# Gates and results of a dense FFN loaded in a step of their own, three chunks ahead, with four places each

## The chip, the cores and the metric

The kernel runs on one core of one Trainium2 chip. The metric is the device time of one execution in microseconds (us), lower is better. Engines are named as in the profile: PE (TensorE matmuls), PEld (TensorE weight loads), DVE (VectorE), ACT (ScalarE), POOL (GpSimd) and SP (SyncE, which issues nearly all loads and stores of this kernel; its rows read SPq). L714 is line 714 of the kernel.

## The reference

A two-layer diffusion transformer for 256 latent and 256 context tokens of width 1024. Each layer has an attention mixer and then a PEER feed-forward part: a product-key router picks 16 of 16,384 experts for each of 8 heads, each expert being one row of `u` and one row of `v`.

```python
idx = jnp.take_along_axis(cand_i.reshape(PEER_CHUNK, PEER_HEADS, PEER_TOPK * PEER_TOPK), best_j, axis=-1)
g = jax.nn.softmax(best_s, axis=-1)
a = jnp.einsum('td,thkd->thk', t, u[idx])
w = (jax.nn.gelu(a.astype(jnp.float32)) * g).astype(t.dtype)
return jnp.einsum('thk,thkd->td', w, v[idx])
```

In layer 0 this is done for latent and context tokens, in layer 1 (the last) for latent tokens alone.

## The kernel before

**Dense experts.** The kernel does not gather experts for the latent tokens. It writes a table of gates (tokens by 16,384 experts, mostly zeros) to DRAM, multiplies the tokens with all of `u` (the U stage), multiplies the results elementwise with the gates and the product with all of `v` (the V stage). All this is `dense()`, once per layer. A value is split into a high and a low part, and each product is three matmuls (high by high, low by high, high by low). In layer 0 a part of the context tokens' experts is gathered row by row beside it: POOL issues the gathers (`row`), DVE multiplies and accumulates them (`gacc`, L576).

**U stage.** 32 chunks of 512 experts, 48 matmuls each. SP loads `du` (4 x 512 KB per chunk, three places in the pool `uphase`), ACT and DVE split it into `duh` and `dul`. The results of a number of chunks stay in SBUF (`dy`), those of the others are stored to DRAM (`ad`) and read back in the V stage.

**V stage.** 64 chunks of 256 experts, in the order `cs`: first the kept ones (16 in layer 0, 22 in layer 1), then those "away" (48 in layer 0, 42 in layer 1). A chunk n has these steps: SP loads its gates `dg` (L706; 384 KB in layer 0, 256 KB in layer 1), its results `dyl` if they are away (L710, 256 KB), and two tiles of V's rows `dv` (L714, 512 KB each). ACT makes `dvh` (L724), DVE makes `dvl` from it (L725). DVE multiplies results by gates in place (L746, "the product" below, M(n)); PE transposes the product (L733), ACT and DVE split it into `dwh` (L737) and `dwl` (L738). Then 24 matmuls in layer 1, or 36 in layer 0, accumulate in PSUM (L753 to L755). `dv`, `dg` and `dyl` have three places each in the pool `vphase`.

**What sets the order.** The program is written chunk by chunk (`v_prep`, `load_v`, `w_prep`, `v_mm`), but each engine's static list of instructions is fixed when the kernel is built, by a scheduler that takes instructions by priority and by when it expects them ready. A load can be listed as soon as its place is free. The pools are put into SBUF by size: `vphase` is opened when `uphase` is closed, and lies in a gap of the memory below it as far as the gap reaches, and in the buffers of `uphase` beyond that. The gap is 67,200 bytes a partition in layer 0 and 63,616 in layer 1; `vphase` takes 64,512 and 57,344. So V's loads may be issued while U still runs, and some are. Loads of SP start in the listed order: one that waits for its place holds up all behind it.

Of the kernel before, what the change touches and what calls it, by code (L numbers as in the profile page):

```python
# [8 lines left out]
F32 = mybir.dt.float32  # L9
# [8 lines left out]
P = 128  # L18
D = 1024
# [8 lines left out]
NC = 64  # L28
# [121 lines left out]
class Builder:  # L150
# [481 lines left out]
    def dense(self, l, tables, hs, ups, yp, keep, mid, late, fin, ad, beside):  # L632

        nc, V, S, G, T = self.nc, self.V, self.S, self.G, self.T
        U = self.A[f"peer_uT{l}"]  # L640
        Vt = self.A[f"peer_v{l}"].rearrange("(c j) d -> c j d", j=P)
        nt = tables.shape[0]
        away = 2 * (NC // 2 - keep)
        cs = list(range(away, NC)) + list(range(away))
        ut, vs, ldv, gts, ys = {}, {}, {}, {}, {}
        up = ups.enter_context(self.pool("uphase", side="right"))

        def u_prep(c):
            if c >= NC // 2:
                return  # L650
            h, l_ = ut.setdefault(c, ([], []))
            for q in range(4):
                t = up.tile([P, 2, UN], F32, name="du", bufs=3)
                nc.sync.dma_start(t, U[c, :, q * 2:(q + 1) * 2])
                th = up.tile([P, 2, UN], F32R, name="duh", bufs=5)
                tl = up.tile([P, 2, UN], F32R, name="dul", bufs=5)
                S.activation(th, t, AF.Copy)  # L657
                with self.tc.high_priority():
                    V.tensor_tensor(tl, t, th.bitcast(F32), ALU.subtract)  # L659
                h += [th[:, 0, :], th[:, 1, :]]  # L660
                l_ += [tl[:, 0, :], tl[:, 1, :]]

        def u_mm(c):

            uh, ul = ut.pop(c)
            w = self.wide() if c % 2 else None
            bs = [w[:, i * 512:(i + 1) * 512] if c % 2 else self.bank("x") for i in range(2)]
            for k in range(KT):
                for (hi, lo), b in zip(hs, bs):
                    T.matmul(b, lhsT=hi[:, k, :], rhs=uh[k], start=k == 0, stop=False)  # L670
                    T.matmul(b, lhsT=hi[:, k, :], rhs=ul[k], start=False, stop=False)  # L671
                    T.matmul(b, lhsT=lo[:, k, :], rhs=uh[k], start=False, stop=k == KT - 1)  # L672
            if 2 * c < away:
                y = up.tile([P, 2, UN], F32, name="da", bufs=2)
            else:
                y = yp.tile([P, 2, UN], F32, name="dy", bufs=keep)
            if c % 2:
                S.activation(y.rearrange("p i n -> p (i n)"), w, AF.Gelu_apprx_tanh)
            else:
                for i in range(2):  # L680
                    S.activation(y[:, i, :], bs[i], AF.Gelu_apprx_tanh)
            if 2 * c < away:
                nc.sync.dma_start(ad[:, :, c * UN:(c + 1) * UN].rearrange("i p n -> p i n"), y)
            else:
                for hf in range(2):
                    ys[2 * c + hf] = y[:, :, hf * 256:(hf + 1) * 256]

        u_prep(0)
        mid()
        for c in range(NC // 2):  # L690
            u_mm(c)
            u_prep(c + 1)
            beside(c)
        ups.close()
        with self.pool("vphase") as vp:
            w = self.wide()
            pacc = [w[:, 0:512], w[:, 512:1024], self.bank("y"), self.bank("y")]
            if nt == 3:
                pacc = [self.bank("x"), self.bank("x")] + pacc[2:] + pacc[:2]

            def load_v(n):
                if n >= NC:
                    return
                c = cs[n]
                gt = vp.tile([P, nt, 256], F32, name="dg", bufs=3)
                nc.sync.dma_start(gt, tables[:, :, c * 256:(c + 1) * 256].rearrange("i p n -> p i n"))  # L706
                gts[n] = gt
                if c < away:
                    ys[c] = vp.tile([P, 2, 256], F32, name="dyl", bufs=3)
                    nc.sync.dma_start(ys[c], ad[:, :, c * 256:(c + 1) * 256].rearrange("i p n -> p i n"))  # L710
                ldv[n] = []
                for a in range(2):
                    t = vp.tile([P, D], F32, name="dv", bufs=3)
                    nc.sync.dma_start(t, Vt[2 * c + a])  # L714
                    ldv[n].append(t)

            def v_prep(n):
                if n >= NC:
                    return
                vh, vl = [], []  # L720
                for v in ldv.pop(n):
                    th = vp.tile([P, D], F32R, name="dvh", bufs=3)
                    tl = vp.tile([P, D], F32R, name="dvl", bufs=3)
                    S.activation(th, v, AF.Copy)  # L724
                    V.tensor_tensor(tl, v, th.bitcast(F32), ALU.subtract)  # L725
                    vh.append(th)
                    vl.append(tl)
                vs[n] = vh, vl

            def w_split(name, src, m):  # L730
                b = self.bank("c", m * P)
                for a in range(m):
                    T.transpose(b[:, a * P:(a + 1) * P], src(a), self.ident)  # L733
                wh = vp.tile([P, m, P], F32R, name=name + "h", bufs=2)
                wl = vp.tile([P, m, P], F32R, name=name + "l", bufs=2)
                b2 = b.rearrange("p (a t) -> p a t", a=m)
                S.activation(wh, b2, AF.Copy)  # L737
                V.tensor_tensor(wl, b2, wh.bitcast(F32), ALU.subtract)  # L738
                return wh, wl

            def w_prep(c):
                if c >= NC:
                    return
                y = ys.pop(cs[c])
                g = gts.pop(c)
                V.tensor_tensor(y, y, g[:, 0:2, :], ALU.mult)  # L746
                ws[c] = [w_split("dw", lambda a: y[:, a // 2, a % 2 * P:a % 2 * P + P], 4)]
                if nt == 3:
                    ws[c].append(w_split("dx", lambda a: g[:, 2, a * P:(a + 1) * P], 2))

            def mm(b, w, a, v, first, last):
                wh, wl = w[0][:, a, :], w[1][:, a, :]
                T.matmul(b, lhsT=wh, rhs=v[0], start=first, stop=False)  # L753
                T.matmul(b, lhsT=wh, rhs=v[1], start=False, stop=False)  # L754
                T.matmul(b, lhsT=wl, rhs=v[0], start=False, stop=last)  # L755

            def v_mm(c):
                vh, vl = vs.pop(c)
                w = ws.pop(c)

                for a, i, hf in [(a, i, hf) for a in range(2) for i in range(nt) for hf in range(2)]:
                    hs = slice(hf * 512, (hf + 1) * 512)
                    mm(pacc[2 * i + hf], w[i // 2], 2 * (i % 2) + a, (vh[a][:, hs], vl[a][:, hs]),
                       c == 0 and a == 0, c == NC - 1 and a == 1)

            ws = {}
            load_v(0)
            v_prep(0)
            load_v(1)
            w_prep(0)  # L770
            for c in range(NC):
                v_prep(c + 1)
                load_v(c + 2)
                w_prep(c + 1)
                v_mm(c)
                next(late, None)
                beside(NC // 2 + c)
            for _ in late:
                pass
            fin(pacc, vp)  # L780

    def ffn(self, l, modT, h, wp, wclose, keep, nt=2, late=iter(()), finish=None, beside=lambda c: None):

        self.tables = tables = self.dr.tile([nt, P, P * P], F32, name=f"table{l}")
        ad = self.dr.tile([2, P, P * P], F32, name=f"ad{l}")
        dense = [tuple(t[:, :, i * P:(i + 1) * P] for t in h) for i in range(2)]
        with self.pool("ypool") as yp:
# [15 lines left out]

            def fin(pacc, vp):

                self.tmp = Slots((yp, "dy", keep), (vp, "dv", 3))
                g = self.gate(modT, 5, 1, "c", self.tmp, None, None)
                y = self.tmp.tile([P, D], F32, name="yadd")
                for i in range(2):
                    self.add_ffn(2 + i, pacc[2 * i:2 * i + 2], g, y)  # L810
                if finish is not None:
                    finish(pacc[4:])
# [281 lines left out]
```

## Time and profile before

| | |
|---|---|
| median of 3 runs | 2890.41 us (2883.72 to 2892.33) |
| the profiled execution | 2891.71 us, its span 2889.9 us |
| mean granted TensorE clock | 0.965 of full |
| PE busy | 2610.9 us, 90% of the span |
| DMA | 735.49 MB, mean 255 GB/s |
| V stage of layer 0, from the last U matmul | 1097.1 to 1666.4 us |
| V stage of layer 1, from the last U matmul | 2438.3 us to some 2870 us |

Busy time is time in which an engine worked on an instruction; shares are of the span. The sum of a prediction is made against the profiled execution and then moved to the median, which lies 1.3 us lower. What a stage is bound by is read from its own stretch, not from the total.

### The profile page before, as it was taken

How to read it: one execution, taken by the hardware profiler on the slowest of the kernel's cores; microseconds unless marked ns; L12 is line 12 of the kernel's file. 1: busy time of each engine (PE TensorE's matmuls, PEld its weight loads, DVE VectorE, ACT ScalarE, POOL GpSimd, SP SyncE). 2: the span in 40 equal slices, each digit the busy share in tenths (PEclk: the TensorE clock that was granted, in tenths of full speed). 3: DMA queues.
4: the chain of work that ended last, by engine and by line, in shares of the span. 5: the costliest groups of instructions: out<-in, count | busy, mean ns of one | idle time of the engine just before them, and what ended most of it. 6: DMA issues, size and time to landing. Idle time of an engine off the chain costs nothing.

```text
span 2889.9 us, 40187 instructions
## 1 busy us (share of the span) xinstructions
PE 2610.9 (90%) x14161; PEld 2134.2 (74%) x14161; DVE 2038.6 (71%) x3904; ACT 1310.6 (45%) x2226; POOL 562.0 (19%) x531
## 2 busy tenths in 40 slices
PE   6999984689999989999999969988999999998786
PEld 4776954567777767888888867868888887886665
DVE  3335699999988877887787874766998555554454
ACT  3334432358673433333333334544599743443332
POOL 0000003343433444433344430000000000000000
PEclk9999997899999999999999979999999999999999
DMA  6453466899999999999999856233778975566664
GB/s 246 132 204 86 160 243 206 278 353 345 354 374 354 358 360 351 351 351 351 338 340 358 316 184 231 91 107 127 238 223 266 313 251 180 180 205 214 201 220 140
DMA packets 354634, 735.49 MB, mean 255 GB/s; under 512 B 35312, under 2 KB 182016, under 8 KB 351872
## 3 DMA queue, kind: packets, MB, share of 16 engines
q1 hardware_dynamic: 299136, 531.56, 54.9%
q0 software_dynamic: 55296, 201.35, 19.5%
q8 instruction: 112, 1.84, 0.3%
q14 instruction: 90, 0.74, 0.1%
HBM read 664.13 MB, written 68.68 MB: 254 GB/s over the span
## 4 chain that ended last, share of the span: by engine, by line
PE 50%; issue 16%; DMA 15%; DVE 9%; POOL 6%; ACT 3%; SPq 1%; DVEq 0%; POOLq 0%; ACTq 0%
DMA dyl<-ad 7%; POOL row L549 5%; PE bank L754 4%; PE bank L755 4%; PE bank L207 4%; PE bank L206 4%; PE bank L753 4%; PE bank L208 4%; DMA du<-in_peer_uT 2%; PE bank L671 2%; PE bank L672 2%; PE wide L755 2%; PE wide L754 2%; PE wide L753 2%; PE bank L670 2%
## 5 line engine op out<-in xcount | busy, mean ns | idle before, releaser
L549 POOL DMA_INDIRECT row<-in_peer_u,gidx x256 | 346.7, 1354 | 530.2 <-DVE row L564 423.8
L724 ACT ACTIVATE dvh<-dv 128x1024 fp32r<-128x1024 f32 x256 | 269.4, 1059 | 393.6 <-DMA dv<-in_peer_v 193.6
L657 ACT ACTIVATE duh<-du 128x1024 fp32r<-128x1024 f32 x256 | 271.1, 1062 | 273.3 <-DMA du<-in_peer_uT 217.9
L659 DVE TENSOR_TENSOR dul<-du,duh 128x1024 fp32r<-128x1024 f32 x256 | 310.4, 1218 | 106.6 <-ACT duh L657 105.5
L725 DVE TENSOR_TENSOR dvl<-dv,dvh 128x1024 fp32r<-128x1024 f32 x256 | 309.2, 1222 | 93.0 <-ACT dvh L724 92.9
L564 DVE SCALAR_TENSOR_TENSOR row<-row,hc 128x1024 f32<-128x1024 f32 x256 | 307.3, 1216 | 22.0 <-DMA row<-in_peer_u,gidx 21.6
L754 PE MATMUL bank<-dvl,dwh 128*128 128x512 f32 x768 | 300.9, 392 | 0.5 <-DVE dvl L725 0.5
L755 PE MATMUL bank<-dvh,dwl 128*128 128x512 f32 x768 | 299.8, 392 | 0.0
L188 DVE TENSOR_TENSOR wl<-wt,wh 128x512 fp32r<-128x512 f32 x256 | 177.9, 700 | 157.9 <-ACT wh L187 155.5
L753 PE MATMUL bank<-dvh,dwh 128*128 128x512 f32 x768 | 265.6, 398 | 2.2 <-ACT dvh L724 1.7
L670 PE MATMUL bank<-duh,h 128*128 128x512 f32 x512 | 197.0, 411 | 65.2 <-ACT duh L657 65.1
L187 ACT ACTIVATE wh<-wt 128x512 fp32r<-128x512 f32 x256 | 160.8, 631 | 205.7 <-PE bank L207 98.9
L671 PE MATMUL bank<-dul,h 128*128 128x512 f32 x512 | 213.9, 418 | 11.9 <-DVE dul L659 11.7
L671 PE MATMUL wide<-dul,h 128*128 128x512 f32 x512 | 209.0, 408 | 10.9 <-DVE dul L659 10.9
L549 POOL DMA_INDIRECT row<-in_peer_v,gidx x128 | 170.5, 1332 | 243.7 <-DVE gacc L576 223.7
L670 PE MATMUL wide<-duh,h 128*128 128x512 f32 x512 | 207.0, 404 | 7.5 <-ACT duh L657 7.4
L206 PE MATMUL bank<-h,wh 128*128 128x256 f32 x704 | 206.0, 294 | 5.4 <-ACT hf L342 5.4
L672 PE MATMUL bank<-duh,h 128*128 128x512 f32 x512 | 208.1, 406 | 0.0
L208 PE MATMUL bank<-h,wl 128*128 128x256 f32 x704 | 204.0, 291 | 3.6 <-DVE wl L188 3.6
L207 PE MATMUL bank<-h,wh 128*128 128x256 f32 x704 | 204.5, 291 | 1.1 <-DVE h L349 1.1
L672 PE MATMUL wide<-duh,h 128*128 128x512 f32 x512 | 203.5, 397 | 0.0
L255 POOL TENSOR_TENSOR rs_t<-rstd 128x2 f32<-128x2 f32 (+1 forms) x27 | 7.4, 273 | 936.0 <-DVE rstd L253 934.7
(279 smaller groups left out, 5905.5 us busy)
## 6 DMA issues: line engine op xcount, KB each, us to landing
du<-in_peer_uT SPq DMA_DIRECT2D x256, 512.0 KB, 6.0
dv<-in_peer_v SPq DMA_DIRECT2D x256, 512.0 KB, 5.7
table<-gst SPq DMA_DIRECT2D x80, 512.0 KB, 7.0
wm<-in_w_mod SPq DMA_DIRECT2D x56, 512.0 KB, 6.9
wt<-in_peer_w_q SPq DMA_DIRECT2D x96, 256.0 KB, 3.3
dg<-table SPq DMA_DIRECT2D x64, 384.0 KB, 7.0
ad<-da SPq DMA_DIRECT2D x45, 512.0 KB, 5.4
dyl<-ad SPq DMA_DIRECT2D x90, 256.0 KB, 5.4
```

Of the source, the lines that this page charges most:

```text
L206: self.T.matmul(out, lhsT=a, rhs=b, start=k == 0 and m == 0, stop=False)
L207: self.T.matmul(out, lhsT=a, rhs=b2, start=False, stop=False)
L208: self.last = self.T.matmul(out, lhsT=a2, rhs=b, start=False, stop=k == KT - 1 and m == len(outs) - 1).ins
L549: self.G.indirect_dma_start(out=t, out_offset=None, in_=table, in_offset=bass.IndirectOffsetOnAxis(ap=idx[:, s:s + 1], axis=0))
L659: V.tensor_tensor(tl, t, th.bitcast(F32), ALU.subtract)
L670: T.matmul(b, lhsT=hi[:, k, :], rhs=uh[k], start=k == 0, stop=False)
L671: T.matmul(b, lhsT=hi[:, k, :], rhs=ul[k], start=False, stop=False)
L672: T.matmul(b, lhsT=lo[:, k, :], rhs=uh[k], start=False, stop=k == KT - 1)
L725: V.tensor_tensor(tl, v, th.bitcast(F32), ALU.subtract)
L753: T.matmul(b, lhsT=wh, rhs=v[0], start=first, stop=False)
L754: T.matmul(b, lhsT=wh, rhs=v[1], start=False, stop=False)
L755: T.matmul(b, lhsT=wl, rhs=v[0], start=False, stop=last)
```

## The change

`load_v` is left with V's rows alone. A new step `load_g` loads gates and results; the loop calls it for chunk c + 3, behind `load_v(c + 2)`. `dv`, `dg` and `dyl` have four places each instead of three. The temporaries that follow the V stage reuse four `dv` places instead of three. All lines behind it move by up to 7 (L710 becomes L709, L714 becomes L717, L725 becomes L728, L746 becomes L749).

```diff
+            def load_g(n):
+                if n >= NC:
+                    return
+                c = cs[n]
+                gts[n] = vp.tile([P, nt, 256], F32, name="dg", bufs=4)
+                nc.sync.dma_start(gts[n], tables[:, :, c * 256:(c + 1) * 256].rearrange("i p n -> p i n"))
+                if c < away:
+                    ys[c] = vp.tile([P, 2, 256], F32, name="dyl", bufs=4)
+                    nc.sync.dma_start(ys[c], ad[:, :, c * 256:(c + 1) * 256].rearrange("i p n -> p i n"))
+
             def load_v(n):
                 if n >= NC:
                     return
-                c = cs[n]
-                gt = vp.tile([P, nt, 256], F32, name="dg", bufs=3)
-                nc.sync.dma_start(gt, tables[:, :, c * 256:(c + 1) * 256].rearrange("i p n -> p i n"))
-                gts[n] = gt
-                if c < away:
-                    ys[c] = vp.tile([P, 2, 256], F32, name="dyl", bufs=3)
-                    nc.sync.dma_start(ys[c], ad[:, :, c * 256:(c + 1) * 256].rearrange("i p n -> p i n"))
                 ldv[n] = []
                 for a in range(2):
-                    t = vp.tile([P, D], F32, name="dv", bufs=3)
-                    nc.sync.dma_start(t, Vt[2 * c + a])
+                    t = vp.tile([P, D], F32, name="dv", bufs=4)
+                    nc.sync.dma_start(t, Vt[2 * cs[n] + a])
                     ldv[n].append(t)
...
             ws = {}
             load_v(0)
+            load_g(0)
+            load_g(1)
+            load_v(1)
+            load_g(2)
             v_prep(0)
-            load_v(1)
             w_prep(0)
             for c in range(NC):
                 v_prep(c + 1)
                 load_v(c + 2)
+                load_g(c + 3)
                 w_prep(c + 1)
                 v_mm(c)
...
-                self.tmp = Slots((yp, "dy", keep), (vp, "dv", 3))
+                self.tmp = Slots((yp, "dy", keep), (vp, "dv", 4))
```

A fourth place of `dv` is 4,096 bytes a partition, one of `dyl` 2,048, one of `dg` 3,072 in layer 0 and 2,048 in layer 1. `vphase` becomes 73,728 bytes in layer 0, 6,528 more than the gap, and 65,536 in layer 1, 1,920 more than the gap.

**Place 1: SP, the end of layer 0's U stage.** Before, the loads of V's first chunks stand between the last `du` loads:

```order
L654 DMA du<-in_peer_uT 128x1024 x2
L706 DMA dg<-table_4361 128x3x256
L714 DMA dv<-in_peer_v 128x1024 x2
L654 DMA du<-in_peer_uT 128x1024
L706 DMA dg<-table_4361 128x3x256
L714 DMA dv<-in_peer_v 128x1024
L706 DMA dg<-table_4361 128x3x256
L710 DMA dyl<-ad_4362 128x2x256 x2
L654 DMA du<-in_peer_uT 128x1024
...
L654 DMA du<-in_peer_uT 128x1024 x17
```

Of the change, the same place:

```order
L654 DMA du<-in_peer_uT 128x1024 x23
L717 DMA dv<-in_peer_v 128x1024 x2
L706 DMA dg<-table_4361 128x3x256 x2
L717 DMA dv<-in_peer_v 128x1024 x2
L706 DMA dg<-table_4361 128x3x256 x2
L926 DMA xl_9945<-xd_74 128x1024
...
L709 DMA dyl<-ad_4362 128x2x256
L717 DMA dv<-in_peer_v 128x1024
L709 DMA dyl<-ad_4362 128x2x256 x3
```

All 23 `du` loads now stand ahead of the first `dv`, and this `dv` waits for the last matmul of U, since its place reaches into the buffers of `uphase`. In layer 1 the list changes in the same way: before, 21 gates, three results and six `dv` stand ahead of the last `du`; now the last `du` is followed by `dv` x2, `dg` x2, `dv` x2, `dg` x2 and then `dyl`, behind the same wait.

**Place 2: SP and DVE, away chunks of layer 1.** The names are numbered: `dv_24735` is the second `dv` of chunk 48, `dv_24783` and `dv_24785` those of chunk 49, `dv_24833` and `dv_24835` those of chunk 50. SP before, where `dyl_24881` is the result of chunk 51 and `dyl_24931` that of chunk 52:

```order
L710 DMA dyl_24881<-ad1_17939 128x2x256
L714 DMA dv_24785<-in_peer_v1 128x1024
L706 DMA dg_25029<-table1_17938 128x2x256
L714 DMA dv_24833<-in_peer_v1 128x1024
L710 DMA dyl_24931<-ad1_17939 128x2x256
```

SP with the change, where `dyl_24889` is the result of chunk 52 and `dyl_24939` that of chunk 53:

```order
L709 DMA dyl_24889<-ad1_17939 128x2x256
L717 DMA dv_24833<-in_peer_v1 128x1024
L706 DMA dg_25087<-table1_17938 128x2x256
L717 DMA dv_24835<-in_peer_v1 128x1024
L709 DMA dyl_24939<-ad1_17939 128x2x256
```

DVE before, at the same chunks:

```order
L746 TENSOR_TENSOR dyl_24881<-dyl_24881,dg_24879 128x512
L725 TENSOR_TENSOR dvl_24776<-dv_24735,dvh_24775 128x1024
L725 TENSOR_TENSOR dvl_24822<-dv_24783,dvh_24821 128x1024
L738 TENSOR_TENSOR dwl_24844<-bank_24838,dwh_24843 128x512
L746 TENSOR_TENSOR dyl_24931<-dyl_24931,dg_24929 128x512
```

DVE with the change:

```order
L749 TENSOR_TENSOR dyl_24889<-dyl_24889,dg_24887 128x512
L728 TENSOR_TENSOR dvl_24780<-dv_24735,dvh_24779 128x1024
L728 TENSOR_TENSOR dvl_24826<-dv_24783,dvh_24825 128x1024
L741 TENSOR_TENSOR dwl_24848<-bank_24842,dwh_24847 128x512
L749 TENSOR_TENSOR dyl_24939<-dyl_24939,dg_24937 128x512
```

The pattern of each engine is the same; products and results stand one chunk further ahead of V's rows than before. Before, `dv_24833` takes the place of `dv_24735` (three places), with the change `dv_24835` does (four places).

**Place 3: DVE, the end of layer 0's V stage.** Here `yadd`, `yctx` and `xl` add the FFN to the residual streams, `gacc` rows are the gathered experts, and `xn` begins the next layer's norm. Before:

```order
L725 TENSOR_TENSOR dvl<-dv,dvh 128x1024
L576 SCALAR_TENSOR_TENSOR gacc<-row,ijgc,gacc 128x1024 x7
L583 TENSOR_TENSOR yadd<-bank,gate 128x512
...
L253 TENSOR_SCALAR rstd<-ss 128x2
L584 TENSOR_TENSOR xl_9945<-xl_9945,yctx 128x512 x2
L576 SCALAR_TENSOR_TENSOR gacc<-row,ijgc,gacc 128x1024 x2
L332 TENSOR_SCALAR xn<-xl_9947,rstd 128x1024
```

With the change:

```order
L728 TENSOR_TENSOR dvl<-dv,dvh 128x1024
L576 SCALAR_TENSOR_TENSOR gacc<-row,ijgc,gacc 128x1024 x8
L583 TENSOR_TENSOR yadd<-bank,gate 128x512
...
L253 TENSOR_SCALAR rstd<-ss 128x2
L584 TENSOR_TENSOR xl_9947<-xl_9947,yctx 128x512 x2
L576 SCALAR_TENSOR_TENSOR gacc<-row,ijgc,gacc 128x1024 x6
L332 TENSOR_SCALAR xn<-xl_9949,rstd 128x1024
```

Behind the last `dvl` and ahead of `xn` there were 15 `gacc` rows (7, six single ones where lines are left out, 2) and are now 20 (8, six, 6).

## Rows read from the trace of the kernel before

**Rows 1.** The page, busy time, share and count of each engine.

```profile
PE 2610.9 (90%) x14161; PEld 2134.2 (74%) x14161; DVE 2038.6 (71%) x3904; ACT 1310.6 (45%) x2226; POOL 562.0 (19%) x531
```

**Rows 2.** Windows: stretch, us, PE, PEld, DVE, ACT, POOL, granted clock, DMA share, GB/s.

```profile
2446.00:2565.00 119.00, 119.00 (x565) 98.36 (x564) 61.22 (x61) 52.16 (x61) 0.00 (x0) 1.00 0.58 181
2565.00:2870.00 305.00, 263.46 (x1196) 206.01 (x1195) 148.18 (x165) 109.36 (x126) 0.00 (x0) 1.00 0.64 206
```

**Rows 3.** Waits in 2565 to 2880: total us, times, longest.

```profile
DVE dyl L746 <- DMA dyl<-ad: 144.5, 39, 5.8
...
SPq L706 <- DVE dyl L746: 165.5, 36, 6.7
```

**Rows 4.** Timeline of SP, away chunks of layer 1: start, us, instruction.

```profile
2577.88 0.39 SPq L710 DMA_DIRECT2D dyl<-ad  x1
...
2652.94 0.39 SPq L710 DMA_DIRECT2D dyl<-ad  x1
...
2845.61 0.38 SPq L710 DMA_DIRECT2D dyl<-ad  x1
```

**Rows 5.** Timeline of DVE there; in brackets idle time ahead and its releaser.

```profile
2650.66 0.69 DVE L746 TENSOR_TENSOR dyl<-dyl,dg 128x512 f32<-128x512 f32 x1 [3.83 <-DMA dyl<-ad]
2651.28 2.35 DVE L725 TENSOR_TENSOR dvl<-dv,dvh 128x1024 fp32r<-128x1024 f32 x2
...
2658.13 0.69 DVE L746 TENSOR_TENSOR dyl<-dyl,dg 128x512 f32<-128x512 f32 x1 [3.90 <-DMA dyl<-ad]
```

**Rows 6.** Timeline of PE, layer 1: transposes of two kept chunks, three chunks apart.

```profile
2446.39 0.60 PE L733 MATMUL bank<-c_ident,dy 128*128 128x128 f32 x4
...
2464.16 0.60 PE L733 MATMUL bank<-c_ident,dy 128*128 128x128 f32 x4
```

**Rows 7.** Timeline of PE, layer 1: from the last U matmul to the first of V.

```profile
2437.93 0.39 PE L672 MATMUL wide<-duh,h 128*128 128x512 f32 x1
2438.16 1.04 PE L733 MATMUL bank<-c_ident,dy 128*128 128x128 f32 x8
2439.92 0.50 PE L753 MATMUL wide<-dvh,dwh 128*128 128x512 f32 x1 [0.73 <-ACT dwh L737]
```

**Rows 8.** All `dg` loads of the kernel: issue to landing.

```profile
DMA to landing us min/median/max: 2.6/4.8/16.9
```

**Rows 9.** Window in layer 0's V, behind several short stalls; columns as in Rows 2.

```profile
1120.00:1130.00 10.00, 7.95 (x27) 6.29 (x26) 9.89 (x16) 2.72 (x3) 4.06 (x3) 0.66 1.05 389
```

**Rows 10.** Timeline of SP, the end of layer 0's U stage.

```profile
990.48 3.75 SPq L654 DMA_DIRECT2D du<-in_peer_uT  x2
...
1024.03 57.21 SPq L654 DMA_DIRECT2D du<-in_peer_uT  x17
```

**Rows 11.** Timeline of PE, layer 0: V matmuls within U, first behind U.

```profile
1081.85 0.42 PE L753 MATMUL bank<-dvh,dwh 128*128 128x512 f32 x1
...
1086.00 0.40 PE L671 MATMUL wide<-dul,h 128*128 128x512 f32 x1
...
1098.24 0.50 PE L753 MATMUL wide<-dvh,dxh 128*128 128x512 f32 x1 [1.11 <-ACT dy L678]
```

**Rows 12.** Timeline of SP, steady V stage of layer 0.

```profile
1195.50 0.38 SPq L706 DMA_DIRECT2D dg<-table  x1
...
1213.19 0.38 SPq L706 DMA_DIRECT2D dg<-table  x1
```

**Rows 13.** Timeline of DVE, the end of layer 0's V stage.

```profile
1655.55 3.92 DVE L576 SCALAR_TENSOR_TENSOR gacc<-row,ijgc,gacc 128x1024 f32<-128x1024 f32 x3
...
1667.45 1.28 DVE L576 SCALAR_TENSOR_TENSOR gacc<-row,ijgc,gacc 128x1024 f32<-128x1024 f32 x1 [1.31 <-DMA row<-in_peer_v,gidx]
...
1683.10 2.59 DVE L576 SCALAR_TENSOR_TENSOR gacc<-row,ijgc,gacc 128x1024 f32<-128x1024 f32 x2
1688.27 1.42 DVE L332 TENSOR_SCALAR xn<-xl,rstd 128x1024 f32<-128x1024 f32 x2 [2.57 <-POOL rstd L258]
```

**Rows 14.** Timeline of PE there: the first matmul behind the V stage's end.

```profile
1689.07 1.97 PE L337 MATMUL bank<-c_ident,xn 128*128 128x128 f32 x8 [22.72 <-DVE xn L332]
```

## The prediction

> **What bounds the kernel now.** I began with the page: PE is busy for 90% of the span [rows 1], so a gain has to come out of the idle tenth. I then looked for the stretches where PE idles and the change touches what it waits for. In layer 1's V stage the windows show both cases side by side [rows 2]: over the kept chunks PE is busy for 119 of 119 us, over the away chunks for 263.46 of 305 us, at full granted clock in both. The DMA share is 0.58 and 0.64, so transfers are not short of bandwidth on the mean. The period says the same: three kept chunks take 2464.16 - 2446.39 = 17.77 us, 5.92 each [rows 6]; away chunks take (2845.61 - 2577.88) / 36 = 7.44 us [rows 4]. The 1.52 us over 39 chunks that wait are 59 us, all that this stretch can give.
>
> The waits name the cause [rows 3]: the product waits for `dyl` 39 times, 144.5 us in all. One round shows how the wait feeds itself [rows 4, 5]. M(n) starts at 2650.66 and ends, for the next instruction, at 2651.28 (0.62). The first of two `dvl` behind it takes half of 2.35, 1.18 (to 2652.46), and frees a place of `dv`. Only then can SP issue the `dv` that stands ahead of the next `dyl`, and then `dyl` at 2652.94 (0.48). M(n+1) starts at 2658.13, when it has landed (5.19). The sum is 7.47 us, the period. So it is a loop: product, `dvl`, `dv` issue, `dyl` issue, landing, product. PE takes no part in it.
>
> **The change, part by part.**
>
> *The steady loop of layer 1.* More places help only if they take an edge out of the loop. With the change SP's list has the same pattern; `dyl` of chunk 53 stands behind the second `dv` of chunk 50, which takes the place (the fourth back) of the second `dv` of chunk 48. Its `dvl` stands on DVE right behind M(52). Before, `dyl` of chunk 52 stood behind the first `dv` of chunk 50, which took the place (the third back) of the same `dv`, whose `dvl` stood right behind M(51). The fourth place has been spent on letting products run one chunk further ahead; every edge is still there, with the same instructions and the same transfers between them. I cost the period at no change, 7.44 us. One round fewer waits, because one result more is loaded in advance: -1.5 us.
>
> A rule points the other way. The Trainium skill, "Perfetto Trace Analysis", section "Optimization Strategy", says that the same gap repeating on the engine that should be saturated can mean that there is no room for the next tile to be allocated, and names the buffer count. By it the 59 us would go. SP's longest wait agrees at first sight: `dg` waits 165.5 us for a product to free its place [rows 3]. But that wait is a step of the loop, released by the same M(n) as `dvl`.
>
> *The start of V in layer 1.* The larger pool makes the first `dv` wait for U's last matmul. That matmul starts at 2437.93 and ends 0.39 later, at 2438.3; the first V matmul starts at 2439.92, so the seam costs 1.6 us now [rows 7], because gates, products and V's rows were made during U. With the change, behind 2438.3: two `dv` issues (0.39 each, taken from a `dyl` issue [rows 4], 0.8), a `dg` that lands in 4.8 (its median [rows 8]), a product of 0.7 [rows 5], transposes and `dwh`: 1.76 from 2438.16 to 2439.92, less 0.44 because four transposes take 0.60 and eight 1.04 [rows 6, 7], 1.3. Sum 7.6, so +6.0. A `dg` at its minimum of 2.6 makes it +3.8; at the maximum, 16.9, +18.1, but I expect the median, since no gathers run in layer 1. Nothing hides it: no matmul is left in U.
>
> After such a gap the clock may fall. The nearest row is a window of layer 0 behind short stalls, at a granted 0.66, between the levels of 1.2 and 2.4 GHz: 0.34 x 7.95 us of busy PE = 2.7 us lost [rows 9]. Bounds 0 and 3.4; I take 2.7. The first chunks then want their loads in one heap: sixteen `dv`, 26 `dg` and three `dyl` in some eight chunks, 16 MB. The kept chunks' window moved 181 GB/s at a share of 0.58, so up to some 312 GB/s by estimate [rows 2]: 51 us, against 8 x 5.92 + 7.6 = 55. Just covered; I take 1 us, bounds 0 and 4. Layer 1 in all: 6.0 + 2.7 + 1.0 - 1.5 = **+8.2**.
>
> *The start of V in layer 0.* Here something is given back. U is bound by transfers at its end. Six `du` issues from 990.48 to 1024.03 took 33.5 us, because V's loads stood between them; the next 17 took 57.21, from the start of the first to the end of the last, (57.21 - 0.39) / 16 = 3.55 each, with 0.39 for one issue [rows 4, 10]. Six at 3.55 are 21.3, so U's loads come 12.2 us earlier. V matmuls that stood in U leave it as well, among them those from 1081.85 to 1086.00, 4.15 us, which lie on PE behind the last `du` [rows 11]. U ended at 1098.24 - 1.11 = 1097.1 [rows 11]; it should end near 1080.7.
>
> Against it stand a gap like that of layer 1, but with gathers and four `xl` loads beside it and 384 KB gates: I take 12 us, between 7.6 (layer 1's) and 18.8 (the `dg` maximum). V has all 64 chunks ahead of it instead of 63, at (1213.19 - 1195.50) / 2 = 8.85 us [rows 12]: 566.1 instead of 557.2. V ended at 1689.07 - 22.72 = 1666.4 [rows 14], so it lost 1666.4 - 1097.1 - 557.2 = 12.1 us to stalls and clock; with chunks that start in order I take 9. So 1080.7 + 12 + 566.1 + 9 = 1667.8: **+1**, rounded down, bounds -8 (gap 7.6, loss 4) and +9 (gap 17, loss 12).
>
> *The end of V in layer 0.* PE stands idle for 22.72 us until `xn` [rows 14], while DVE works off gathered rows and adds. Five more `gacc` rows now stand there. The 15 rows of before took 1655.55 to 1685.69 with all that is between, 2.0 us each [rows 13]; alone one is 3.92 / 3 = 1.3, and one that waits for its gather 1.31 + 1.28 = 2.6 [rows 13]. One stands ahead of the first `yadd`, on the gather's pace: 2.6. Four stand behind `rstd`; there DVE idled 2.57 us for POOL [rows 13], which hides as much: 4 x 2.0 - 2.57 = 5.4. Together **+8.0**, bounds 1.3 + 4 x 1.3 - 2.57 = 3.9 and 2.6 + 4 x 2.6 - 2.57 = 10.4. That POOL now puts gathers between the steps of the `rstd` chain lies inside these bounds.
>
> The rest costs nothing: `Slots` with a fourth `dv` place only widens the choice of memory behind V, and the steady V of layer 0 stays bound by PE at 8.85 us, which is above the loop's 7.44.
>
> Sum: 8.2 + 1 + 8.0 = +17.2 on 2891.7, 2908.9; the median lies 1.3 lower, so **2908**.
>
> **The rivals.**
>
> *A: the deeper buffers do break the loop.* If SP issues `dyl` well before M(n) runs, because the list drifts or because landing, not the loop, sets the pace, the period falls to PE's 5.92. For it: transfers are at a share of 0.64 only, and the product waits nearly every time. Against it: the edges read from the two lists are the same. It decides if `dyl` comes more than 1.52 us earlier against the loop. Then 59 less, with starts and end as above: 2908 + 1.5 - 59 = 2850. By the page's rule this is the expected case. I give 12%.
>
> *B: the costs are hidden.* Layer 0's start gains its 8 us, its end costs 3.9, layer 1 costs 6.0 - 1.5 = 4.5 with a clock that holds: about 0, so 2890. For it: gathers and clock have wide bounds. Against it: all three have to come out low. 17%.
>
> *C: the starts collide.* Loads of layer 0 land late behind gathers and `xl` (+9), its end takes 10.4, layer 1 falls behind in its first chunks (+13): +32, so 2923. For it: `dg` took up to 16.9 us. 13%.
>
> **How the numbers follow.** The forecast has 58%. About 0.3%, 8.7 us, is what a measurement of this kernel can tell from no change: 2881.7 and 2899.1. A is faster, B lies within, and one in fifty of the forecast's cases too; some of B's spread falls under 2881.7. That gives 0.13 faster, 0.17 same, 0.70 slower. The range leaves out A and the upper part of C: 2884 to 2926; the forecast's own is 2899 to 2918.
>
> **What would show it.** Right: the `dyl` period of layer 1 stays at 7.4 us, with about as long waits of M for `dyl`; a gap of some 7 us of PE behind the last U matmul of layer 1, and some 12 behind that of layer 0, which ends near 1081; PE idle for some 30 us instead of 22.72 at layer 0's end. Wrong: a `dyl` period under 7 us, or an issue of `dyl` whose landing is long past when M starts; or a first `dv` that is issued while U still runs.

## The result: 0.6% slower, the loop untouched, layer 0 paying most

The kernel with the change took 2905.47 us (median of 6 runs, 2901.06 to 2911.50) against 2891.32 us (median of 6 runs, 2883.72 to 2897.25): +14.2 us between the medians. The ratio is 1.0061 with a 95% interval of 1.0047 to 1.0076, which is some 18 us, 14 to 22. Forecast were 2908 us and +17. The profiled execution took 2903.53 us, its span is 2901.8.

The first thing to look at is whether the loop of layer 1 is still there. Windows of the changed kernel, over kept chunks and then away chunks (columns as in [rows 2]):

```profile
2475.00:2585.00 110.00, 110.00 (x522) 90.70 (x520) 66.12 (x72) 48.59 (x57) 0.00 (x0) 1.00 0.69 227
2585.00:2870.00 285.00, 249.52 (x1132) 195.25 (x1132) 143.20 (x160) 104.91 (x122) 0.00 (x0) 1.00 0.67 215
```

PE is busy for 88% of the away chunks, as before (86% in [rows 2]). The waits of the changed kernel in 2565 to 2880 (total us, times, longest) answer to [rows 3]:

```profile
ACT dvh L727 <- PE bank L758: 193.3, 89, 3.7
DVE dyl L749 <- DMA dyl<-ad: 135.4, 38, 4.3
```

The product waits for `dyl` 38 times instead of 39, 3.6 us each time (3.7 before). What has gone is ACT's wait for V's rows, which before, in the same stretch, was

```profile
ACT dvh L724 <- DMA dv<-in_peer_v: 174.2, 72, 6.4
```

With the change `dvh` waits for PE to free its place, so `dv` lands in time, and nothing is gained by it. SP's timeline shows the same round as [rows 4]:

```profile
2697.55 0.33 SPq L717 DMA_DIRECT2D dv<-in_peer_v  x1
2697.98 0.38 SPq L709 DMA_DIRECT2D dyl<-ad  x1
2698.77 0.33 SPq L717 DMA_DIRECT2D dv<-in_peer_v  x1
2703.76 0.38 SPq L706 DMA_DIRECT2D dg<-table  x1
2704.89 0.33 SPq L717 DMA_DIRECT2D dv<-in_peer_v  x1
2705.31 0.39 SPq L709 DMA_DIRECT2D dyl<-ad  x1
```

and DVE's timeline the product that waits, with the two `dvl` right behind it, as [rows 5]:

```profile
2695.69 0.69 DVE L749 TENSOR_TENSOR dyl<-dyl,dg 128x512 f32<-128x512 f32 x1 [3.69 <-DMA dyl<-ad]
2696.30 2.35 DVE L728 TENSOR_TENSOR dvl<-dv,dvh 128x1024 fp32r<-128x1024 f32 x2
...
2703.04 0.69 DVE L749 TENSOR_TENSOR dyl<-dyl,dg 128x512 f32<-128x512 f32 x1 [3.78 <-DMA dyl<-ad]
```

From one `dyl` issue to the next it is 2705.31 - 2697.98 = 7.33 us; from the first product that waits to the last, 7.25 us on the mean, against 7.39 before, measured in the same way.

The seams are where time was lost. PE of layer 1, from the last U matmul, answers to [rows 7]:

```profile
2448.22 0.40 PE L672 MATMUL wide<-duh,h 128*128 128x512 f32 x1
2455.30 1.12 PE L736 MATMUL bank<-c_ident,dy 128*128 128x128 f32 x4 [6.68 <-DVE dy L749]
```

PE waits 6.68 us for the first product. On DVE this product stands behind the first `dvl`, which waits until `dv` has landed and ACT has made `dvh`; the product itself then starts without a wait:

```profile
2453.42 1.23 DVE L728 TENSOR_TENSOR dvl<-dv,dvh 128x1024 fp32r<-128x1024 f32 x1 [16.40 <-ACT dvh L727]
2454.56 0.68 DVE L749 TENSOR_TENSOR dy<-dy,dg 128x512 f32<-128x512 f32 x1
```

In layer 0 SP now issues U's last loads in one go (19 of them in the stretch shown), and V's first rows behind them (to [rows 10]). PE shows the gap in front of V (to [rows 11]), and DVE's first product does wait for its gates there:

```profile
1002.54 61.86 SPq L654 DMA_DIRECT2D du<-in_peer_uT  x19
1077.70 0.80 SPq L717 DMA_DIRECT2D dv<-in_peer_v  x2
1078.55 1.13 SPq L706 DMA_DIRECT2D dg<-table  x2
```

```profile
1091.97 1.11 PE L736 MATMUL bank<-c_ident,dy 128*128 128x128 f32 x4 [14.30 <-DVE dy L749]
...
1093.77 0.79 PE L756 MATMUL bank<-dvh,dwh 128*128 128x512 f32 x1 [0.26 <-ACT dwh L740]
```

```profile
1091.23 0.69 DVE L749 TENSOR_TENSOR dy<-dy,dg 128x512 f32<-128x512 f32 x1 [2.87 <-DMA dg<-table]
```

At the end of layer 0's V stage PE is idle for longer than in [rows 14], and DVE's timeline (to [rows 13]) shows why:

```profile
1679.42 1.29 DVE L584 TENSOR_TENSOR xl<-xl,yctx 128x512 f32<-128x512 f32 x2
1680.63 3.92 DVE L576 SCALAR_TENSOR_TENSOR gacc<-row,ijgc,gacc 128x1024 f32<-128x1024 f32 x3
1685.26 1.28 DVE L576 SCALAR_TENSOR_TENSOR gacc<-row,ijgc,gacc 128x1024 f32<-128x1024 f32 x1 [0.71 <-DMA row<-in_peer_v,gidx]
1690.82 1.28 DVE L576 SCALAR_TENSOR_TENSOR gacc<-row,ijgc,gacc 128x1024 f32<-128x1024 f32 x1 [4.27 <-DMA row<-in_peer_v,gidx]
1693.34 1.28 DVE L576 SCALAR_TENSOR_TENSOR gacc<-row,ijgc,gacc 128x1024 f32<-128x1024 f32 x1 [1.24 <-DMA row<-in_peer_v,gidx]
1694.54 1.42 DVE L332 TENSOR_SCALAR xn<-xl,rstd 128x1024 f32<-128x1024 f32 x2
```

```profile
1695.35 0.90 PE L337 MATMUL bank<-c_ident,xn 128*128 128x128 f32 x3 [32.33 <-DVE xn L332]
```

Between `xl` and `xn` there are six gathered rows, and DVE waits for three of them. The wait of 4.27 us is for a gather whose issue stands on POOL behind the steps of the `rstd` chain. POOL's timeline:

```profile
1684.96 0.19 POOL L255 TENSOR_TENSOR rs_t<-rstd 128x2 f32<-128x2 f32 x1
1685.23 0.19 POOL L256 TENSOR_TENSOR rs_t<-rs_t,ss 128x2 f32<-128x2 f32 x1
1685.93 1.47 POOL L549 DMA_INDIRECT row<-in_peer_v,gidx  x1 [0.51 <-issue]
```

Laid end to end by the first and last matmul of each stage, the two profiled executions differ like this (us):

| stretch | before | after | difference |
|---|---|---|---|
| up to layer 0's first U matmul | 524.9 | 519.6 | -5.3 |
| U of layer 0 | 572.2 | 558.1 | -14.1 |
| last U to first V matmul, layer 0 | 1.1 | 16.1 | +15.0 |
| V of layer 0 behind it | 567.4 (63 chunks) | 568.4 (64) | +1.0 |
| last V matmul of layer 0 to `xn` on PE | 23.5 | 33.2 | +9.7 |
| from there to layer 1's first U matmul | 329.6 | 333.6 | +4.0 |
| U of layer 1 | 419.6 | 419.7 | 0 |
| last U to first V matmul, layer 1 | 1.6 | 9.2 | +7.6 |
| V of layer 1 behind it | 432.0 | 426.0 | -6.0 |
| the rest | 18.0 | 18.0 | 0 |

The sum is 11.9, the difference of the spans. The first line lies ahead of everything that the change touches; over the runs below it varies between 519.0 and 525.0. So the change itself costs 17 in this pair of executions.

### The profile page after: what moved, and what is told of

It reads as the page before. It is cut to its first block, busy times and chain, and to the rows that moved or that the text cites. A ratio compares the mean times of both kernels' runs of the same rounds, so it can differ in the third digit from the quotient of the medians.

```text
span 2901.8 us, 40158 instructions
## 1 busy us (share of the span) xinstructions
PE 2610.4 (90%) x14161; PEld 2139.2 (74%) x14161; DVE 2041.5 (70%) x3904; ACT 1311.6 (45%) x2226; POOL 543.8 (19%) x531
## 4 chain that ended last, share of the span: by engine, by line
PE 33%; issue 24%; DMA 16%; DVE 12%; POOL 9%; ACT 4%; SPq 1%; POOLq 0%; DVEq 0%; ACTq 0%
POOL row L549 9%; DMA dyl<-ad 6%; PE bank L206 3%; PE bank L207 3%; PE bank L208 3%; PE bank L628 2%; DMA du<-in_peer_uT 2%; DVE dul L659 2%; DMA wm<-in_w_mod 2%; PE wide L672 2%; PE wide L671 2%; PE wide L670 2%; PE bank L671 2%; PE bank L672 2%; PE bank L670 2%
## 5 line engine op out<-in xcount | busy, mean ns | idle before, releaser
L728 DVE TENSOR_TENSOR dvl<-dv,dvh 128x1024 fp32r<-128x1024 f32 x256 | 310.1, 1223 | 172.2 <-ACT dvh L727 172.1
L756 PE MATMUL bank<-dvh,dwh 128*128 128x512 f32 x768 | 298.1, 399 | 0.7 <-ACT dvh L727 0.5
L671 PE MATMUL bank<-dul,h 128*128 128x512 f32 x512 | 212.6, 415 | 10.7 <-DVE dul L659 10.4
L549 POOL DMA_INDIRECT row<-in_peer_v,gidx x128 | 158.1, 1235 | 250.5 <-DVE gacc L576 223.4
```

Of the source, the lines that this page charges most:

```text
L549: self.G.indirect_dma_start(out=t, out_offset=None, in_=table, in_offset=bass.IndirectOffsetOnAxis(ap=idx[:, s:s + 1], axis=0))
```

## The experiments

All ratios are to the kernel before, run on the same chip. The stretches are taken from each run's profile as in the table above.

**Is it the places or the step?** The old loading step with four places of each:

```diff
-                gt = vp.tile([P, nt, 256], F32, name="dg", bufs=3)
+                gt = vp.tile([P, nt, 256], F32, name="dg", bufs=4)
...
-                    ys[c] = vp.tile([P, 2, 256], F32, name="dyl", bufs=3)
+                    ys[c] = vp.tile([P, 2, 256], F32, name="dyl", bufs=4)
...
-                    t = vp.tile([P, D], F32, name="dv", bufs=3)
+                    t = vp.tile([P, D], F32, name="dv", bufs=4)
...
```

(Here and in the runs below, `Slots` names as many `dv` places as the run has.)

> The old loading step (gates, results and V's rows of a chunk together), but four places of each, so the pool is as large as in the change. Theory (the larger pool makes V's first loads wait for U's end, and gathered rows pile up at layer 0's end, 19 gacc rows ahead of xn): PE gap of 6 to 7 us behind layer 1's U and some 14 us behind layer 0's U, dyl period 7.2 to 7.5 us, about 2900 to 2908. Rival (the separate step three chunks ahead is what costs): starts as before, without gaps, 2888 to 2894.

Measured: 2902.73 us, ratio 1.0059 (1.0038 to 1.0080). The places alone cost what the change costs. From U's last matmul to V's first it is 8.9 us in layer 0 (expected some 14; here the gates stand ahead of V's rows in SP's list) and 5.8 in layer 1. Layer 0's V stage behind it takes 576.4 us, 8.0 more than with the change, so both starts come out alike. PE is idle for 31.9 us at layer 0's end.

**The step alone**, the change with three places of each:

```diff
-                gts[n] = vp.tile([P, nt, 256], F32, name="dg", bufs=4)
+                gts[n] = vp.tile([P, nt, 256], F32, name="dg", bufs=3)
...
-                    ys[c] = vp.tile([P, 2, 256], F32, name="dyl", bufs=4)
+                    ys[c] = vp.tile([P, 2, 256], F32, name="dyl", bufs=3)
...
-                    t = vp.tile([P, D], F32, name="dv", bufs=4)
+                    t = vp.tile([P, D], F32, name="dv", bufs=3)
...
```

> The new loading step of the change with three places of each, so the pool fits the gap as before. Theory: six V rows are loaded ahead of U's end in each layer, no gap behind U, 15 gacc rows ahead of xn, dyl period 7.3 to 7.5 us because the loop of product, dvl, dv issue, dyl issue is there unchanged: 2885 to 2895. Rival (the separate step costs by itself): 2900 to 2908. Rival (the separate step brings results earlier): dyl period under 7 us, under 2875.

Measured: 2883.26 us, ratio 1.0000 (0.9983 to 1.0017). The period is 7.21 us, the seam of layer 1 is 1.6 us again, PE idle at layer 0's end 21.9. A loading step of its own is worth nothing and costs nothing that these runs can tell (some 5 us either way).

**Is it the size of the pool?** The kernel before, with a tile more in the pool that nothing reads:

```diff
         with self.pool("vphase") as vp:
+            pad = vp.tile([P, 2304 if nt == 3 else 2048], F32, name="dpad", bufs=1)
+            V.memset(pad[:, 0:1], 0.0)
```

> The kernel before with its three places and its old step; the pool of the V stage has one more tile that nothing reads (9,216 bytes a partition in layer 0, 8,192 in layer 1; one small memset of it on DVE per layer), so it is as large as in the change. Theory (size alone moves V's first loads behind U's last matmul, the fourth places are not needed for it): PE gaps behind both U stages as with the change (13 to 16 and 6 to 9 us), no V matmul within U; 14 gacc rows ahead of xn in its list, so PE idle of 20 to 23 us at layer 0's end; dyl period 7.4 us; ratio 1.000 to 1.004. Rival (places, not size, move the loads): V's loads within U, ratio 1.000, no gaps.

Measured: 2901.04 us, ratio 1.0045 (1.0028 to 1.0062), a little above the expected range. Size alone pushes V's loads behind U: SP of this run issues the first of them 0.03 us after layer 1's last U matmul, which ends at 2447.11.

```profile
2447.14 0.38 SPq L708 DMA_DIRECT2D dg<-table  x1
2447.57 0.94 SPq L716 DMA_DIRECT2D dv<-in_peer_v  x2
```

The gaps are 10.9 us (13 to 16 expected) and 6.1 us. With 14 gathered rows ahead of `xn`, PE idles for only 19.7 us, but layer 0's V stage takes 583.4 us. It loses most of the difference at its start, where PE is idle more and has a lower granted clock than with the change (this run first, then the change):

```profile
1096.00:1150.00 54.00, 46.61 (x199) 37.47 (x199) 39.33 (x61) 18.97 (x27) 15.27 (x13) 0.87 1.01 373
1094.00:1150.00 56.00, 55.52 (x265) 45.91 (x266) 41.54 (x64) 21.41 (x31) 13.14 (x12) 0.98 1.02 377
```

So a pool that is too large costs time with fewer rows at the end too, in another place.

**One layer at a time.** The change with four places in one layer and three in the other; the first of the two runs has them in layer 0:

```diff
-                gts[n] = vp.tile([P, nt, 256], F32, name="dg", bufs=4)
+                gts[n] = vp.tile([P, nt, 256], F32, name="dg", bufs=4 if nt == 3 else 3)
```

(`dyl` and `dv` alike; in the other run 3 and 4 change places.)

> The change with four places in layer 0 and three in layer 1. Theory, from the trace of the change: layer 0 carries nearly all of the cost, about +2 at its start (U 14 us shorter, a PE gap of some 15 us) and +10 at its end (20 gacc rows ahead of xn, PE idle for 32 us instead of 22.7), with some 3 us more ahead of layer 1's U: ratio 1.003 to 1.006. Rival (the prediction's split: 9 of layer 0, 8 of layer 1): ratio 1.003 too, but then the run with four places in layer 1 alone is at 1.003 as well.

> The change with three places in layer 0 and four in layer 1. Theory, from the trace of the change: a PE gap of 6 to 9 us behind layer 1's U, given back by some 6 us fewer waits in its V stage; ratio 0.999 to 1.002. Rival (the prediction's split): +8, ratio 1.003.

Measured: four places in layer 0, 2904.33 us, ratio 1.0061 (1.0045 to 1.0078); in layer 1, 2893.09 us, ratio 1.0014 (1.0002 to 1.0027). The split in the prediction was wrong: layer 0 costs some 18 us and layer 1 some 4. (Their sum lies above the change's 18; the intervals allow that.)

**Does the loop run through SP's list?** The results of layer 1 are loaded from POOL's queue, in the change and, with the same edit, in the kernel before:

```diff
-                    nc.sync.dma_start(ys[c], ad[:, :, c * 256:(c + 1) * 256].rearrange("i p n -> p i n"))
+                    (nc.sync if nt == 3 else nc.gpsimd).dma_start(ys[c], ad[:, :, c * 256:(c + 1) * 256].rearrange("i p n -> p i n"))
```

> The changed kernel, in which the results of layer 1 (dyl) are loaded from POOL's queue, so that no dv issue stands ahead of them; all else alike. Theory (the loop runs through SP's list): the product no longer waits for dvl of the product before; the remaining round goes over two chunks (product, dvl, matmuls, transposes that free the place, dyl issue, landing: 0.6 + 1.2 + 2.8 + 0.6 + 0.5 + 5.0 = 10.7 us, 5.4 a chunk), so PE's 5.92 us a chunk binds; V of layer 1 loses up to 47 us less, 2858 to 2870. Rival (landing of the results or bandwidth sets the pace, not the order): period stays above 7 us, 2895 to 2910.

> The kernel before (three places, old step), with the results of layer 1 loaded from POOL's queue. Theory: as in the run with the change, the period falls from 7.4 to 5.9 to 6.2 us with three places too, because the places were not what was short: 2838 to 2855. Rival (the fourth place is needed as well): period above 6.8 us, 2870 to 2892.

Measured: 2859.05 us, ratio 0.9913 (0.9880 to 0.9946) with the change, and 2836.16 us, ratio 0.9826 (0.9799 to 0.9853) without it. One edge out of the loop gives 50 us with three places; layer 1's V stage falls from 432.0 to 380.9 us, and with the change from 426.0 to 380.5. POOL's timeline of the faster one has one `dyl` per 5.93 us:

```profile
2654.56 0.72 POOL L710 DMA_DIRECT2D dyl<-ad  x1 [5.18 <-PE bank L733]
2660.49 0.72 POOL L710 DMA_DIRECT2D dyl<-ad  x1 [5.21 <-PE bank L733]
```

and windows of it show PE busy for 369 of 370 us of layer 1's V stage, and for 254 of 255 over its away chunks:

```profile
2450.00:2820.00 370.00, 369.15 (x1745) 304.84 (x1744) 209.19 (x223) 159.84 (x184) 28.25 (x39) 1.00 0.70 227
2565.00:2820.00 255.00, 254.15 (x1202) 209.78 (x1201) 149.96 (x165) 109.35 (x126) 28.25 (x39) 1.00 0.75 247
```

Before, the away chunks moved 206 GB/s at a DMA share of 0.64 [rows 2]; here 247 at 0.75. Bandwidth did not set the period. Nor is it a faster landing on the other queue: from a `dyl` issue to the product, where it waits for that load, the mean is 4.5 us here and 5.1 before, which is 0.5 of the 1.5 us that a chunk gained. The product still waits for `dyl` nearly every time, in 2565 to 2830, but PE no longer waits with it:

```profile
DVE dyl L746 <- DMA dyl<-ad: 57.0, 37, 4.7
```

**More places still.** The kernel before with six places in layer 1, of `dyl` in the first run and of `dv` in the second:

```diff
-                    ys[c] = vp.tile([P, 2, 256], F32, name="dyl", bufs=3)
+                    ys[c] = vp.tile([P, 2, 256], F32, name="dyl", bufs=3 if nt == 3 else 6)
```

> The kernel before with six places of dyl in layer 1 (all else as before; the pool still fits the gap). Theory: products run three chunks further ahead in DVE's list, and each dyl still stands behind a dv whose dvl stands right behind the product before, so the dyl period stays at 7.2 to 7.5 us: ratio 0.997 to 1.002. Rival (there were too few places for the results): period near 5.9 us, ratio 0.982 to 0.986.

> The kernel before with six places of dv in layer 1 (the pool then reaches into U's buffers in layer 1). Theory: dyl of the next chunk stands behind the dv that the dvl right behind the last product sets free, whatever the number of places; period 7.2 to 7.5 us, a gap of 6 to 9 us behind layer 1's U: ratio 1.000 to 1.004. Rival (too few places for V's rows): period near 5.9 us, ratio under 0.99.

Measured: 2884.74 us, ratio 0.9993 (0.9981 to 1.0005), period 7.25 us; and 2890.77 us, ratio 1.0011 (0.9996 to 1.0026), period 7.28 us. Twice the places of either kind leave the period where it was (the edit for `dv` is alike). The waits of the run with six `dv` show it again:

```profile
DVE dyl L746 <- DMA dyl<-ad: 140.0, 39, 4.7
```

**The end of layer 0.** Five of 128 gathered rows of `v` left out, in the change and in the kernel before:

```diff
-        for s in range(P):
+        for s in range(P - 5):
             t = self.gather(gp, self.A[f"peer_v{l}"], idx, s)
```

> The changed kernel without the last five of the 128 gathered rows of v (five experts of the context tokens are left out): 17 instead of 20 gacc rows ahead of xn. Theory (PE idle at layer 0's end goes with these rows, some 2.1 us each): 25 to 28 us instead of 32.3, ratio to the kernel before 1.002 to 1.005. Rival (the idle time comes from the order of POOL's rstd steps and gathers): it stays above 30 us.

> The kernel before without the same five rows: 11 instead of 15 gacc rows ahead of xn. Theory: PE idle of 13 to 16 us instead of 22.7, ratio 0.996 to 0.998. Rival (something other than the rows ends the wait, such as the rstd chain on POOL): 20 us or more.

Measured: 2893.81 us, ratio 1.0025 (1.0012 to 1.0037), PE idle 25.2 us, inside the theory's range. This does not exclude the rival, for without the five rows POOL's `rstd` steps also run with no gather between them, and DVE waits for none behind `rstd`. From `rstd` to `xn` DVE takes 6.4 us before, 15.2 with the change and 7.8 in this run (`rstd` of the three, then `xn` of this run; the other two `xn` stand in [rows 13] and above):

```profile
1681.83 0.16 DVE L253 TENSOR_SCALAR rstd<-ss 128x2 int32<-128x2 int32 x1
1679.36 0.17 DVE L253 TENSOR_SCALAR rstd<-ss 128x2 int32<-128x2 int32 x1
1683.92 0.16 DVE L253 TENSOR_SCALAR rstd<-ss 128x2 int32<-128x2 int32 x1
1691.70 1.42 DVE L332 TENSOR_SCALAR xn<-xl,rstd 128x1024 f32<-128x1024 f32 x2 [2.58 <-POOL rstd L258]
```

So 8.7 of the 9.7 us that the change loses here lie behind `rstd`, and the number of rows and the place of their gathers on POOL changed together. No run takes the two apart.

The other run: 2878.83 us, ratio 0.9974 (0.9960 to 0.9988), PE idle 20.3 us, where the theory had 13 to 16. There its rival holds: with 11 rows something else ends the wait. DVE's timeline of that run has no gathered row between `xl` and `xn`, and waits for POOL's `rstd` chain. It also has two products and two adds of the finished `gacc`, some 2.4 us, ahead of `xn`, which before stand behind it:

```profile
1676.72 1.28 DVE L583 TENSOR_TENSOR gacc<-gacc,gate 128x512 f32<-128x512 f32 x2
...
1679.12 1.28 DVE L584 TENSOR_TENSOR xl<-xl,gacc 128x512 f32<-128x512 f32 x2
...
1680.39 1.28 DVE L584 TENSOR_TENSOR xl<-xl,yctx 128x512 f32<-128x512 f32 x2
1684.82 1.42 DVE L332 TENSOR_SCALAR xn<-xl,rstd 128x1024 f32<-128x1024 f32 x2 [3.14 <-POOL rstd L258]
```

Over all runs, the `gacc` rows that stand between the last `dvl` and `xn` in DVE's list, and PE's idle time:

```
rows  PE idle (us)
11    20.3
14    19.7
15    21.2 to 22.7 (six runs, the kernel before among them)
16    24.6
17    25.2
19    31.9
20    32.3, 32.4, 33.4 (the change is the first)
```

The two runs with fewer than 15 rows stay near 20 us. Above 15 a row goes with some 2.1 us on the mean, (32.7 - 22.0) / 5, but not evenly: from 17 to 19 rows it is 6.7 us. The four runs with 19 and 20 rows are those in which DVE waits for gathers behind `rstd`, 6.2 to 7.2 us in each.

**A version that fits the gap**, with the results of layer 1 on POOL's queue:

```diff
-                gts[n] = vp.tile([P, nt, 256], F32, name="dg", bufs=4)
+                gts[n] = vp.tile([P, nt, 256], F32, name="dg", bufs=3)
...
-                    nc.sync.dma_start(ys[c], ad[:, :, c * 256:(c + 1) * 256].rearrange("i p n -> p i n"))
+                    (nc.sync if nt == 3 else nc.gpsimd).dma_start(ys[c], ad[:, :, c * 256:(c + 1) * 256].rearrange("i p n -> p i n"))
...
-                    t = vp.tile([P, D], F32, name="dv", bufs=4)
+                    t = vp.tile([P, D], F32, name="dv", bufs=3 if nt == 3 else 4)
```

> The new step with places that fit the gap (layer 0: three dv, three dg, four dyl; layer 1: four dv, three dg, four dyl), and the results of layer 1 loaded from POOL's queue. Theory: V's loads start within U again, no gap at layer 1's U, 16 gacc rows ahead of xn, period 5.92 us: as the kernel before with POOL's queue, ratio 0.980 to 0.985. Rival (fourth places help once the loop is gone): 0.975 or less.

Measured: 2844.57 us, ratio 0.9851 (0.9832 to 0.9870). It beats both kernels and has no gap behind U (1.1 and 1.6 us), but is no faster than the old step with three places on the same queue. The fastest version measured is the kernel before with that one edit; the two intervals overlap.

## Why the prediction was right, and where its terms were not

**The steady loop** was right, and is shown rather than argued: an edge taken out of it gives 50 us, and more places, four of each or six of `dyl` or `dv`, give nothing. Periods with the loop in place range from 7.19 to 7.40 us in the nine other runs that have it; 7.39 in the profile of before is near the top of them, and the kernel before without five rows has the 7.40. So the 6.0 us that layer 1's V stage is shorter in the profile after are not more than this spread, 0.2 us over 38 rounds. What remains is the one wait fewer, as predicted.

**The start of V in layer 1** was predicted at +6.0 for the gap, +2.7 for the clock and +1.0 for the heap of loads. The gap measured +7.6, but not by the path that was added up. The forecast let the landing of the gates end the wait, with 4.8 us, a median over both layers; layer 1's own gates before land in 2.8 us on the median. In the trace the path runs from the first `dv` issue (2448.64) over its landing, `dvh` and `dvl` to the product at 2454.56. The gates were issued at 2449.49 and by the trace landed 4.8 us later, 0.3 us ahead of the product, so both paths are of nearly the same length, and that the sum came near is in part luck. Clock and heap measured less: from V's first matmul to the transposes of the first away chunk it is 125.7 us after (2457.80 to 2583.46) and 124.9 before (2439.92 to 2564.79), +0.8 in place of +3.7. The clock did fall, as the windows of the changed kernel show: behind the gap of 6.68 us a granted 0.69, between the levels of 1.2 and 2.4 GHz, and in the window after it 1.00, the upper one:

```profile
2455.00:2465.00 10.00, 9.08 (x33) 7.27 (x34) 6.53 (x10) 3.20 (x4) 0.00 (x0) 0.69 1.05 376
2465.00:2475.00 10.00, 10.00 (x51) 8.22 (x50) 9.08 (x12) 4.89 (x6) 0.00 (x0) 1.00 1.07 380
```

Part of that loss lies in the gap, whose transposes took 1.12 us instead of 0.60. The layer's sum was predicted at +8.2 and measured at +4 (1 to 8) by the run with four places in layer 1 alone: the term for clock and heap was mis-sized, 3.7 forecast and 0.8 measured.

**The start of V in layer 0** was predicted at +1 and measured +1.9, but by three terms that were off against each other, so that the sum came out is luck. U came 14.1 us shorter (16.4 predicted). The seam was 16.1 us (12): the gates stand behind V's rows in SP's list, and the first product got them 12.7 us behind their issue (1078.55 to 1091.23). V then lost 568.4 - 566.1 = 2.3 us (9). The bound of 18.8 for the seam does not follow from the sum of layer 1, which with a `dg` at its maximum gives 0.8 + 16.9 + 0.7 + 1.3 = 19.7; nothing hangs on it.

**The end of layer 0** was predicted at +8.0 and measured +9.7 from the last V matmul to `xn`, and +4.0 behind it. The step that failed is that the 2.57 us in which DVE had idled for `rstd` would hide as much of the rows' time. POOL's `rstd` steps now stand between gathers, and DVE idles 0.71 + 4.27 + 1.24 = 6.2 us for gathers instead: the rows behind `rstd` cost 8.7 us where 5.4 were forecast, those ahead of it 1.0 where 2.6 were. The prediction held this to lie inside its bounds of 3.9 to 10.4; of the time up to `xn` alone that is so. The 4.0 us ahead of layer 1's U it did not have. The three runs with 20 rows have 333.6 to 334.4 us there, the others, with 11 to 19, from 327.8 to 332.9. So a part of it may come with the rows that are left over and a part is the spread of this stretch; that stays open.

**The rivals.** A (the deeper buffers break the loop) fell, and with it the reading of the repeated gap by the Trainium skill, "Perfetto Trace Analysis", section "Optimization Strategy": the page says that too few buffers can be the cause, and had they been, more places would have closed the gap. Six of either kind left it, so the measurement decides against that cause here. B (costs hidden) fell for layer 0, and came near in layer 1. C (the starts collide) was half seen: layer 0's seam is longer than forecast, but V made it up.

So the total was right to 3 us, but with luck: by the table layer 1 was put too high by 6.6 us (8.2 against 7.6 - 6.0 = 1.6) and layer 0 too low by as much (9.0 against 1.9 + 9.7 + 4.0 = 15.6), and by the runs with one layer alone, too high by some 4 and too low by some 9. The mechanisms, a loop that stays and a pool that starts V late, were right.

## What to carry to other kernels

When a wait repeats at a fixed period, write down the round, from the late instruction back to itself, through the queues as well as the engines. If an issue in it stands behind another whose place the same round sets free, more places only shift the numbering, as four and six did here; a queue of its own for the late load took the round apart with a change of one word. Before a place is added, compare the pool's size with the gap that lets it overlap the stage before. In layer 1 a pool of 63,488 bytes a partition (six `dyl`) still loaded ahead of U's end, with a seam of 1.6 us; one of 65,536, 1,920 over the gap, loaded nothing ahead.

## What the runs showed that I had not expected

The late start of V was forecast; the trace adds that behind the gap it costs layer 1 only 0.8 us, and that layer 0's end costs more than its start. There, four more rows stand behind `rstd` on DVE, their gathers fall between POOL's `rstd` steps, and DVE waits 6.2 us for gathers where it had waited 2.57 us for `rstd`. With fewer than 15 rows behind the last `dvl` PE still idles for some 20 us: the adds and then POOL's `rstd` steps remain, and other adds move ahead of `xn`.
